# A Hymba layer on one core: a new first phase, a new order of products in the last unit, and new constants in the list scheduler

## The chip, the core and the metric

The kernel runs on one core of a Trainium2 chip. The core has five engines that run their own instruction lists in order and wait for each other by semaphores: TensorE (PE in the profile, with its weight loads as PEld), VectorE (DVE), ScalarE (ACT), GpSimd (POOL) and SyncE (SP), which here issues the transfers between the main memory and the on-chip memory. The metric is the device time of one execution in microseconds (us); the number for a kernel is the median of several executions.

## The reference

One decoder layer over 2048 tokens of width 1024, followed by a final RMS norm, all in float32. What matters of it:

```python
mod = silu(c) @ w_ada + b_ada
shift, scale, gate = split(mod, 3)
h = rmsnorm(x, g_norm) * (1 + scale) + shift
gq, gk, gv, ga, gz, sq, sk, sv, sz = split_cols(h @ w_in, COL_SIZES)
log_a = log_sigmoid(ga @ w_decay + b_decay) / 16
o_gla = rmsnorm(gla_chunked(gq, gk, gv, log_a), g_gla_head) * silu(gz)
o_swa = sliding_window_sink_attention(rope(sq), rope(sk), sv, sinks) * silu(sz)
x = x + gate * (concat(o_gla, o_swa) @ w_out)
return rmsnorm(x, g_final)
```

The first three lines are the modulation and the norm. `c` is one row, so `mod` is one row for all tokens. The projection by `w_in` is the largest piece of work; its columns are cut into slots named `sz`, `gz`, `kv`, `gv`, `sq` and `qk`.

## The kernel before, in words

**Tiling.** The 2048 tokens are four units of 512 (`NU`, `NB`). Within a unit the width of 1024 is eight blocks of 128 (`KT`, index k or j). Numbers are split into a high part, rounded to the format fp32r, and the low remainder, and one product becomes three: high by high, low by high, high by low. `hh` and `hl` are the two parts of the modulated, normed h; weights are split in the same way in unit 0, stored to a scratch tensor `wc`, and reloaded by the units 1 to 3. `mmul` (L454 in the profile) issues each matrix product and `trans` (L459) each transposition; a wrapper at L397 issues the operations of the other engines and the transfers.

**What sets the order.** The kernel does not issue directly. The class `Order` records each operation with a modelled duration; `issue` then takes, engine by engine, the operation that can start first by the model and, among those ready, the one with the smallest key. `od.lift` moves keys (a negative lift brings work forward). `begin` holds the model of time: when an engine is free, how fast the transfers (`wire`) go, and how far SyncE may run ahead. All operations of the whole kernel are sorted in this way, so a constant in `begin` can move instructions in any unit. The engines keep the order that comes out.

**The first phase** (unit 0). SyncE loads the small tensors, x transposed (`xT`, into `xt0`), the modulation's weights (`wa`, one tile for each k with a shift half and a scale half) and the first weights (`wr_first`). `warm` issues small products without use (`pw`). `silu_rows` spreads silu(c) over all partitions by 16 small products (`pb`). `norm0_start` squares the eight blocks of x on ScalarE and VectorE, adds them in pairs (`sq`), sums them over the partitions by four products with a matrix of ones (`ss`), and makes 1/rms by two ScalarE activations (log, then exp). The result stands in `ss`, and a copy of it in `rstd`. The second use of `warm` fills TensorE's time behind the sums. `ada_cols` multiplies `wa` by the silu row and adds along the row, on VectorE (two operations a k); ScalarE then makes `ashift` and `amul` of k. `norm0_scale` and `norm0_k` make `hh` and `hl` of one k. For k=1, 3, 5, 7 VectorE multiplies x by `amul` and `rstd` in one operation and ScalarE adds `ashift`. With each k that is finished, `proj_t_outer` issues the products of this k into open sums (`po`).

**The slots.** Each unit runs through a list of slots; `ORDER0` is that of unit 0, `ORDER` that of units 1 and 2, `ORDER_F[3]` that of unit 3 (`FAST` names the units with a fast form). Unit 3 makes `sq` and `gv` together, as slot `sqgv`, with seven block products in place of eight. `SEVEN` lists them, with the block of h or sum of blocks at the left and of the weights at the right: `slot_f` streams their weights (tiles `w_b` from `wc`, tiles `w_t` from sums of weight blocks made before and stored to `wt`), and `proj_f` issues the products (`pf`) and what follows each. The sums of blocks of h (`S`, split to `Shh` and `Shl`) are made by `prepare` and pass through a scratch tensor `sd` on the way. Attention work becomes ready when the slots that it needs are done.

**Late work.** The gate's third of the modulation and the output weights are made in small pieces behind slots of the units 1 and 2; `LATE_AT` says where.

Of the kernel before, what the change touches and what calls it, by code (L numbers as in the profile page):

```python
# [18 lines left out]
P = 128  # L19
# [38 lines left out]
FAST = (3,)  # L58
ORDER_F = {2: ['sz0','kv','sz1','sqgv','qk0','gz0','qk1','gz1'], 3: ['sz0','kv','sqgv','sz1','qk0','gz0','qk1','gz1']}
STATS_AT = 0  # L60
# [3 lines left out]
SEVEN = (("a11", "b11"), ("a12", "b21"), ("s2", "t2"), ("s3", "t3"), ("a22", "t4"), ("s1", "t1"), ("s4", "b22"))  # L64
LATE_AT = {(1,'sz0'):'gate',(1,'sz1'):0,(1,'sq'):4,(1,'gv'):5,(1,'qk1'):6,(2,'sz0'):7,(2,'sz1'):1,(2,'gv'):2,(2,'gz0'):3}
WO = ("b11", "b21", "t1", "b22", "t2", "t3", "t4")
WARM0, WARM = 14, 13
WITH_V = (1, 3, 5, 7)
# [37 lines left out]
class Order:  # L106
# [3 lines left out]
    def __init__(self, tc):  # L110
        self.tc, self.nc = tc, tc.nc
        self.real = {"V": self.nc.vector, "A": self.nc.scalar, "G": self.nc.gpsimd,
                     "PE": self.nc.tensor, "SP": self.nc.sync}
        self.ops, self.tiles, self.rings, self.seen = [], {}, {}, {}
        self.free = dict.fromkeys(self.real, 0.0)
        self.port = self.wire = 0.0
        self.mode = self.cell = None
        self.last = dict.fromkeys(self.real)
        self.busy = {}
        self.group, self.groups = None, 0  # L120
        self.lift = 0
        self.home, self.after_pool, self.users_of = {}, {}, {}
# [195 lines left out]
    def begin(self, o, t):  # L318
        e = o.eng
        if o.bytes:  # L320

            self.wire = max(self.wire, t + 0.9) + o.bytes / (360e3 if t < 20 else 370e3)
            o.start, o.end = t, max(self.wire + 0.9, t + 2.0)
            self.free[e] = max(t + 0.07, self.wire - BACKLOG)
            return
        if e == "PE":
            dur = o.dur
            if o.mode != self.mode:
                t += 0.1
# [73 lines left out]
def layer_kernel(ctx, tc, small, x, xT, w_ada, w_gate, b_gate, w_in, w_dec, w_out, g_fin, out):  # L403
# [37 lines left out]


    def mmul(o, l, r, start, stop, bank=None):
        n, m, k = free_size(r), free_size(l), l.shape[0]
        mode = cell = None
        if l.dtype == F32:
            dur = 2 * max(0.107, n / 1200)
            if k <= 64:
                mode, cell = "rows", l.start_partition()
            elif m <= 64:  # L450
                mode, cell = "cols", o.start_partition()
        else:
            dur = max(0.112, n / 2400 + 0.0137)
        return od.add("PE", lambda: T.matmul(o, l, r, start=start, stop=stop), dur,  # L454
                      [l, r] + ([] if start else [o]), [bank if start and bank is not None else o],
                      mode=mode, cell=cell)
# [84 lines left out]
    def silu_rows():  # L541

        pb = rows.tile([P, D], F32, name="pb")
        for j in range(KT):
            with od.together():
                for i in range(2):
                    mmul(pb[:, j * P:(j + 1) * P], s_p[i][:, j:j + 1].broadcast_to([P, P]), ident_r,
                         i == 0, i == 1)
        return pb

    def ada_load(j):
        wa = begin.tile([P, 2, D], F32, name=f"wa{j}", tag="wa", bufs=WAB)
        was[j] = wa
        if j == 0:
            for i in range(2):
                SY.dma_start(wa[:, i], w_ada[:, j, i])
# [136 lines left out]

    def slot_f(u):

# [15 lines left out]

        stream.extend([lambda n=n, j=j: load(n, j) for n in range(7) for j in range(2)])
        return lambda i, n, k: tiles[n, k // 2][:, k % 2, i]
# [38 lines left out]

    def proj_f(u, w, combos, qr_of):

# [53 lines left out]
        combos, second = combos  # L808
        for n, (a, _) in enumerate(SEVEN):
            if n == STATS_AT and u < NU - 1:  # L810
# [7 lines left out]
            for p in range(2):  # L818
# [6 lines left out]
                done(a, p, ps)  # L825
                od.lift = 0

    def rope_in_place(q, t):
# [159 lines left out]
    def norm0_start():  # L988
# [4 lines left out]
        for j in range(0, KT, 2):  # L993
# [658 lines left out]
    todo = [(0, n) for n in ORDER0] + [(u, n) for u in range(1, NU) for n in (ORDER_F[u] if u in FAST else ORDER)]  # L1652
    ws = [slot_f(u) if n == "sqgv" else slot_w(u, n, LIFT if i > 1 else 0) for i, (u, n) in enumerate(todo)]
    ready_s = {}

    warm(WARM0, None)
    srow = silu_rows()
    norm0_start()
    b1 = const.tile([P, KT], F32, name="b1")
# [54 lines left out]
    for i, (u, slot) in enumerate(todo):  # L1714
# [8 lines left out]
        elif name == "sqgv":  # L1723
            qrs[u] = {}
            proj_f(u, w, ready_s[u], qrs[u])
        elif name == "sq":
# [7 lines left out]
        seen.add((u, slot))  # L1734
        seen |= {(u, n) for n in ("sq", "gv") if name == "sqgv"}
        if half:
# [22 lines left out]
        if u < NU - 1 and name == ("sqgv" if u in FAST else NORM_AT if u else NORM_AT0):  # L1759
            od.lift = -LIFT  # L1760
# [66 lines left out]
```

## Time and profile before

| | us |
|---|---|
| median of 3 runs | 822.41 (822.4 to 823.12) |
| profiled execution, its own time | 822.16 |
| its span, first to last instruction | 820.4 |
| VectorE busy (76% of the span) | 626.8 |
| ScalarE busy (64%) | 528.0 |
| GpSimd busy (46%) | 377.7 |

The span is what the trace covers; the execution's own time holds 1.8 us more around it. The mean granted clock of TensorE is 0.998 over the span. The transfers move 221.79 MB at a mean of 270 GB/s. In a timeline row the first number is the start in the span, the second the time from the first start to the last end of the group, `xN` the number of instructions in it, and the bracket at the end says how long the engine idled before it and what released it. One product of 128x512 in float32 counts as two records.

### The profile page before, as it was taken

The numbers are of one execution on the slowest core, as the hardware profiler recorded it, in microseconds if no ns is written. First come the engines' busy times: TensorE is split into PE (matmuls) and PEld (weight loads), VectorE is DVE, ScalarE is ACT, GpSimd is POOL, SyncE is SP. The second block draws the span as 40 slices with busy tenths as digits, with TensorE's granted clock in tenths as the row PEclk, the third lists the DMA queues.
The fourth block names the chain that finished last, engine by engine and source line by source line (L and its number), as shares of the span: only waits on it lengthen the run. The fifth ranks groups of instructions, "written<-read, shape, count | busy, mean of one in ns | idle before, by whom it ended". The sixth has DMA issues, their size and how long they took to land.

```text
span 820.4 us, 13492 instructions
## 1 busy us (share of the span) xinstructions
PE 803.6 (98%) x4262; PEld 669.0 (82%) x4262; DVE 626.8 (76%) x1234; ACT 528.0 (64%) x1315; POOL 377.7 (46%) x458
## 2 busy tenths in 40 slices
PE   8899999999999999999999999999999999999996
PEld 7788788888888878878887888788888888888885
DVE  6998467777668988675788958877686577989985
ACT  4769856899546787857488766453786636444432
POOL 3813225476435766656569542343644332223300
PEclk9999999999999999999999999999999999999999
DMA  9979998738286597998977967899999945664422
GB/s 357 372 257 379 380 388 290 265 130 325 100 291 233 195 371 251 303 336 307 348 278 269 324 225 235 286 353 402 340 350 346 309 128 178 218 201 153 165 99 78
DMA packets 101917, 221.79 MB, mean 270 GB/s; under 512 B 10531, under 2 KB 28502, under 8 KB 99158
## 3 DMA queue, kind: packets, MB, share of 16 engines
q1 hardware_dynamic: 101558, 220.67, 75.8%
q8 instruction: 34, 0.56, 0.3%
q14 instruction: 37, 0.30, 0.1%
q10 hardware_dynamic: 288, 0.26, 0.1%
HBM read 156.80 MB, written 64.09 MB: 269 GB/s over the span
## 4 chain that ended last, share of the span: by engine, by line
PE 76%; DMA 7%; DVE 4%; ACT 4%; issue 2%; POOL 1%; SPq 1%; DVEq 0%; POOLq 0%; ACTq 0%
PE pt L454 23%; PE pn L454 15%; PE ya L454 10%; PE ys L454 9%; PE pf L454 5%; PE ppo L454 3%; PE psc L454 3%; PE po L454 2%; PE ppt L459 2%; DMA xt<-in_xT 1%; DMA xn<-in_x 1%; PE pc L454 1%; PE pms L454 1%; DMA wr_gv<-in_w_in 1%; PE pu L454 1%
## 5 line engine op out<-in xcount | busy, mean ns | idle before, releaser
L454 PE MATMUL pt<-hh,w_gz 128*128 128x512 f32 x224 | 75.7, 397 | 0.0
L454 PE MATMUL pt<-hh,w_qk 128*128 128x512 f32 x224 | 74.5, 398 | 0.0
L454 PE MATMUL pt<-hh,w_sz 128*128 128x512 f32 x224 | 73.6, 397 | 0.3 <-ACT kvr L397 0.3
L397 ACT ACTIVATE ge<-ge 128x512 f32<-128x512 f32 x96 | 60.5, 630 | 9.8 <-DVE ge L397 8.9
L397 ACT ACTIVATE s<-s,nm 128x129 f32<-128x129 f32 x128 | 51.1, 400 | 18.4 <-DVE nm L397 17.8
L454 PE MATMUL pn<-w_gv,hh 128*128 128x512 f32 x192 | 62.0, 397 | 0.2 <-ACT kvr L397 0.2
L454 PE MATMUL pn<-w_sq,hh 128*128 128x512 f32 x192 | 61.7, 395 | 0.0
L397 POOL TENSOR_TENSOR xt<-xt,rstd 128x512 f32<-128x512 f32 x27 | 40.6, 1505 | 28.7 <-DMA xt<-in_xT 24.9
L454 PE MATMUL ys<-woht,m 128*128 128x512 f32 x168 | 53.6, 392 | 0.0
L397 POOL TENSOR_TENSOR o<-o,zs 128x128 f32<-128x128 f32 x64 | 33.5, 542 | 39.8 <-DVE o L397 29.8
L454 PE MATMUL pn<-w_kv,hh 128*128 128x272 f32 x256 | 50.1, 290 | 0.2 <-ACT zs L397 0.2
L454 PEld LDWEIGHTS pt<-hh,w_sz 128*128 128x128 f32 x224 | 41.7, 188 | 9.2 <-ACT kvr L397 0.5
L454 PE MATMUL ya<-wohb,m 128*128 128x512 f32 x152 | 49.0, 390 | 0.0
L454 PEld LDWEIGHTS pt<-hh,w_gz 128*128 128x128 f32 x224 | 41.7, 188 | 8.5 <-issue 0.2
L454 PEld LDWEIGHTS pt<-hh,w_qk 128*128 128x128 f32 x224 | 41.7, 188 | 8.3
L397 POOL TENSOR_TENSOR s<-s,den 128x512 f32<-128x512 f32 x32 | 37.7, 1181 | 16.1 <-DVE den L397 15.3
L454 PE MATMUL pt<-hl,w_gz 128*128 128x512 f32 x112 | 44.5, 397 | 0.0
L454 PE MATMUL pt<-hl,w_sz 128*128 128x512 f32 x112 | 44.4, 396 | 0.0
L454 PE MATMUL pt<-hl,w_qk 128*128 128x512 f32 x112 | 44.3, 396 | 0.0
L397 POOL TENSOR_TENSOR qr<-qr,rope 128x256 f32<-128x256 f32 x32 | 26.4, 846 | 35.4 <-DVE rope L397 25.7
L454 PEld LDWEIGHTS pn<-w_sq,hh 128*128 128x128 f32 x192 | 35.8, 188 | 8.1 <-issue 0.3
L454 PEld LDWEIGHTS psc<-kst,qs 128*128 128x128 f32 x256 | 37.7, 188 | 5.5 <-DVE s L397 1.0
(324 smaller groups left out, 2475.1 us busy)
## 6 DMA issues: line engine op xcount, KB each, us to landing
w_sz<-wc SPq DMA_DIRECT2D x24, 512.0 KB, 6.2
w_qk<-wc SPq DMA_DIRECT2D x24, 512.0 KB, 5.1
w_gz<-wc SPq DMA_DIRECT2D x24, 512.0 KB, 5.1
w_sq<-wc SPq DMA_DIRECT2D x16, 512.0 KB, 7.0
w_gv<-wc SPq DMA_DIRECT2D x16, 512.0 KB, 9.1
w_t<-wt SPq DMA_DIRECT2D x16, 512.0 KB, 7.4
mr<-mixd SPq DMA_DIRECT2D x32, 256.0 KB, 3.6
y<-in_x SPq DMA_DIRECT2D x32, 256.0 KB, 3.3
```

Source lines behind the costliest of these rows:

```text
L397: return order.add(eng, lambda: real(*args, **kw), dur, ins, outs, lock=lock, nbytes=nbytes)
L454: return od.add("PE", lambda: T.matmul(o, l, r, start=start, stop=stop), dur, [l, r] + ([] if start else [o]), [bank if start and bank is ...
L459: return od.add("PE", lambda: T.transpose(o, i, ident), 0.109, [i, ident], [o], mode="few" if o.shape[0] <= 32 else None)
```

## The change

1. `WARM0` goes from 14 to 5 and `WARM` from 13 to 9. `FILL` puts two small products behind the silu row and behind each of the first three sums. In the planner these first products get longer durations (`cold`).
2. In `ada_load` and `ada_cols` the scale half stands ahead of the shift half, and `amul` follows its half at once.
3. The copy of 1/rms to `rstd` goes from ScalarE to VectorE.
4. The planner's constants: all engines are free from 0.8 us, the first load is costed by itself, the wire runs at 405 GB/s ahead of 20 us in place of 360, and an issue costs 0.45 us ahead of 6 us.
5. Unit 3: `sz1` comes ahead of `sqgv`, and `sqgv` keeps the first five of the seven products (`SPLIT`); the last two become a slot of their own, `gvb`, behind `qk0`. (`ORDER_F[2]` is changed too, but unit 2 is not in `FAST`.)
6. `LATE_AT`: the gate and the first output rows come in one slot, and five other pieces move to other slots of units 1 and 2.

```diff
-ORDER_F = {2: [...], 3: ['sz0','kv','sqgv','sz1','qk0','gz0','qk1','gz1']}
+ORDER_F = {2: [...], 3: ['sz0', 'kv', 'sz1', 'sqgv', 'qk0', 'gvb', 'gz0', 'qk1', 'gz1']}
-LATE_AT = {(1,'sz0'):'gate',(1,'sz1'):0,(1,'sq'):4,(1,'gv'):5,(1,'qk1'):6,(2,'sz0'):7,(2,'sz1'):1,(2,'gv'):2,(2,'gz0'):3}
+LATE_AT = {(1, 'sz0'): ('gate', 0), (1, 'kv'): 4, (1, 'gv'): 5, (1, 'qk1'): 6, (2, 'sz0'): 7, (2, 'kv'): 1, (2, 'qk0'): 2, (2, 'gv'): 3}
-WARM0, WARM = 14, 13
+WARM0, WARM = 5, 9
+FILL = (2,2,2,2)
...
-        self.free = dict.fromkeys(self.real, 0.0)
+        self.free = dict.fromkeys(self.real, 0.8)
...
-            self.wire = max(self.wire, t + 0.9) + o.bytes / (360e3 if t < 20 else 370e3)
+            if not self.wire:
+                self.wire = 2.8
+                o.start, o.end = t, t + 1.75
+                self.free[e] = t + 0.45
+                return
+            self.wire = max(self.wire, t + 0.9) + o.bytes / (405e3 if t < 20 else 370e3)
             o.start, o.end = t, max(self.wire + 0.9, t + 2.0)
-            self.free[e] = max(t + 0.07, self.wire - BACKLOG)
+            self.free[e] = max(t + (0.45 if t < 6 else 0.07), self.wire - BACKLOG)
...
+        od.lift = -LIFT
+        warm(FILL[0], x)
+        od.lift = 0
         return pb
...
         if j == 0:
-            for i in range(2):
+            for i in (1, 0):
                 SY.dma_start(wa[:, i], w_ada[:, j, i])
...
-        for i in range(2):
+        for i in (1, 0):
             V.scalar_tensor_tensor(wa[:, i], wa[:, i], 1.0, srow, op0=ALU.mult, op1=ALU.mult,
                                    accum_out=ada[:, j, i:i + 1])
-        A.activation(ashift[:, j:j + 1], ada[:, j, 0:1], AF.Identity, bias=b_sb[:, j, 0:1])
-        A.activation(amul[:, j:j + 1], ada[:, j, 1:2], AF.Identity, bias=b1[:, j:j + 1], scale=g_sb[:, j:j + 1])
+            if i:
+                A.activation(amul[:, j:j + 1], ada[:, j, 1:2], AF.Identity, bias=b1[:, j:j + 1],
+                             scale=g_sb[:, j:j + 1])
+            else:
+                A.activation(ashift[:, j:j + 1], ada[:, j, 0:1], AF.Identity, bias=b_sb[:, j, 0:1])
...
+    SPLIT = 5
+
+    def part_of(u, slot):
+        at = SPLIT if "gvb" in ORDER_F[u] else len(SEVEN)
+        return range(at) if slot == "sqgv" else range(at, len(SEVEN))
...
             i = mmul(ps, ones, sq[0], j == 0, j == KT - 2)
+            if j < KT - 2:
+                warm(FILL[1 + j // 2], i)
             od.lift = 0
...
-            od.lift = 60
-            A.copy(rstd[0], rstd[1])
-            od.lift = 0
+            V.tensor_copy(rstd[0], rstd[1])
...
+    cold[0] = 0.427
     warm(WARM0, None)
+    cold[0] = 0.17
     srow = silu_rows()
+    cold[0] = 0.0
     norm0_start()
```

What the planner makes of it is seen in the engines' lists. First TensorE's head: behind the first warm-up (one row, x14 before and x5 now) and the silu row's products (`pb`), before:

```order
L454 MATMUL pb<-ident_r,s_cl 128x128
L454 MATMUL ss<-sq_112,ones_r 128x512
L454 MATMUL ss<-sq_114,ones_r 128x512
L454 MATMUL ss<-sq_116,ones_r 128x512
L454 MATMUL ss<-sq_118,ones_r 128x512
L454 MATMUL pw<-ident,ones_r 128x128 x13
L454 MATMUL po_141<-hh_0_149,w_first_123 128x256
```

and now (`pw` are the small products, `ss` the sums; a product's line is L463 in the changed file):

```order
L463 MATMUL pb<-ident_r,s_cl 128x128
L463 MATMUL pw<-ident,ones_r 128x128 x2
L463 MATMUL ss<-sq_113,ones_r 128x512
L463 MATMUL pw<-ident,ones_r 128x128 x2
L463 MATMUL ss<-sq_116,ones_r 128x512
L463 MATMUL pw<-ident,ones_r 128x128 x2
L463 MATMUL ss<-sq_119,ones_r 128x512
L463 MATMUL pw<-ident,ones_r 128x128 x2
L463 MATMUL ss<-sq_122,ones_r 128x512
L463 MATMUL pw<-ident,ones_r 128x128 x9
```

The four sums had stood next to each other; now two small products stand ahead of each. In all there are 22 small products where there were 27.

Second, VectorE from the last pair of squares on, before (`wa` with `ada` is the modulation, two operations a k; the number behind `hl_` or `hh_` is k):

```order
L397 TENSOR_TENSOR sq_118<-sq_118,sq_119 128x512
L397 SCALAR_TENSOR_TENSOR wa_147,ada<-wa_147,pb 128x1024 x2
L397 TENSOR_TENSOR xt_111<-xt_111,ss 128x256 x2
L397 TENSOR_TENSOR hl_0_150<-xt_111,hh_0_149 128x256 x2
L397 SCALAR_TENSOR_TENSOR wa_151,ada<-wa_151,pb 128x1024 x2
L397 SCALAR_TENSOR_TENSOR xt_111<-xt_111,amul,rstd_121 128x512
```

and now:

```order
L403 TENSOR_TENSOR sq_122<-sq_122,sq_123 128x512
L403 SCALAR_TENSOR_TENSOR wa_151,ada<-wa_151,pb 128x1024 x2
L403 TENSOR_TENSOR xt_112<-xt_112,ss 128x256 x2
L403 COPY rstd_125<-ss 128x512
L403 SCALAR_TENSOR_TENSOR wa_155,ada<-wa_155,pb 128x1024 x2
L403 TENSOR_TENSOR hl_0_154<-xt_112,hh_0_153 128x256 x2
L403 SCALAR_TENSOR_TENSOR xt_112<-xt_112,amul,rstd_125 128x512
```

The copy has come in, and the modulation of k=1 has moved ahead of `hl` of k=0. On ScalarE the copy is gone, and `amul` of k=0 stands ahead of the two activations of 1/rms in place of behind them.

Third, SyncE in unit 3, from the loads of the products' first weights on, before (with the buffers' numbers: `S013` to `S313` are the four sums of h that are stored, `w_b113` and `w_b213` the weights of the first two products, `w_t23` those of the third, `w_sz13` those of slot `sz1`):

```order
L397 DMA w_b113_0_1407<-wc_102 128x1024 x2
L397 DMA sd3_104<-S013_1395 128x512
L397 DMA sd3_104<-S113_1397 128x512
L397 DMA w_b113_1_1432<-wc_102 128x1024 x2
L397 DMA w_b213_0_1433<-wc_102 128x1024 x2
L397 DMA w_b213_1_1434<-wc_102 128x1024 x2
L397 DMA sd3_104<-S213_1399 128x512
L397 DMA w_t23_0_1435<-wt_105 128x1024 x2
L397 DMA w_t23_1_1445<-wt_105 128x1024 x2
L397 DMA w_t33_0_1446<-wt_105 128x1024 x2
L397 DMA sd3_104<-S313_1401 128x512
L397 DMA S023_1465<-sd3_104 128x512
```

and now:

```order
L403 DMA sd3_104<-S013_1399 128x512
L403 DMA w_sz13_0_1411<-wc_102 128x1024 x2
L403 DMA sd3_104<-S113_1401 128x512
L403 DMA w_sz13_1_1436<-wc_102 128x1024 x2
L403 DMA w_b113_0_1437<-wc_102 128x1024 x2
L403 DMA sd3_104<-S213_1403 128x512
L403 DMA w_b113_1_1438<-wc_102 128x1024 x2
L403 DMA w_b213_0_1439<-wc_102 128x1024 x2
...
L403 DMA sd3_104<-S313_1405 128x512
L403 DMA S023_1477<-sd3_104 128x512
L403 DMA w_t23_0_1452<-wt_105 128x1024 x2
```

The weights of `sz1` have come ahead of those of the seven products, and the first `w_t` load has moved from ahead of the last store of S to behind it.

More of the change, by code (lines that the diff above doesn't have):

```diff
@@ L58 @@
 FAST = (3,)
-ORDER_F = {2: ['sz0','kv','sz1','sqgv','qk0','gz0','qk1','gz1'], 3: ['sz0','kv','sqgv','sz1','qk0','gz0','qk1','gz1']}
+ORDER_F = {2: ['sz0','kv','sqgv','sz1','qk0','gz0','qk1','gz1'], 3: ['sz0', 'kv', 'sz1', 'sqgv', 'qk0', 'gvb', 'gz0', 'qk1', 'gz1']}
 STATS_AT = 0
@@ L440, in f @@
         return ap.bitcast(F32)
+    cold = [0.0]
     def mmul(o, l, r, start, stop, bank=None):
@@ L453, in mmul @@
             dur = max(0.112, n / 2400 + 0.0137)
+        dur = max(dur, cold[0])
         return od.add("PE", lambda: T.matmul(o, l, r, start=start, stop=stop), dur,
@@ L462, in warm @@
     def warm(n, after):
+        if not n:
+            return
         p = att.tile([P, P], F32, name="pw", tag="pqk")
@@ L468, in warm @@
                 i.deps.add(after)
+        return i
     sm = const.tile([P, SMALL[-1]], F32, name="small")
@@ L546, in silu_rows @@
                 for i in range(2):
-                    mmul(pb[:, j * P:(j + 1) * P], s_p[i][:, j:j + 1].broadcast_to([P, P]), ident_r,
-                         i == 0, i == 1)
+                    x = mmul(pb[:, j * P:(j + 1) * P], s_p[i][:, j:j + 1].broadcast_to([P, P]), ident_r,
+                             i == 0, i == 1)
+        od.lift = -LIFT
+        warm(FILL[0], x)
+        od.lift = 0
         return pb
@@ L692, in late_cols, with slot_f @@
         part("t4", b[1, 0], b[1, 0], b[1, 1])
-    def slot_f(u):
+    SPLIT = 5
+    def part_of(u, slot):
+        at = SPLIT if "gvb" in ORDER_F[u] else len(SEVEN)
+        return range(at) if slot == "sqgv" else range(at, len(SEVEN))
+    def slot_f(u, slot):
         tiles = {}
@@ L710, in load @@
                 SY.dma_start(f(t[:, k]), f(src))
-        stream.extend([lambda n=n, j=j: load(n, j) for n in range(7) for j in range(2)])
+        stream.extend([lambda n=n, j=j: load(n, j) for n in part_of(u, slot) for j in range(2)])
         return lambda i, n, k: tiles[n, k // 2][:, k % 2, i]
@@ L751, in prepare, with proj_f @@
         return combos, second
-    def proj_f(u, w, combos, qr_of):
+    def proj_f(u, combos, qr_of):
         def left(op, k, p):
@@ L808, in proj_f, with product @@
         combos, second = combos
-        for n, (a, _) in enumerate(SEVEN):
+        def product(n, a, w):
             if n == STATS_AT and u < NU - 1:
@@ L826, in proj_f, with run @@
                 od.lift = 0
+        def run(slot, w):
+            for n in part_of(u, slot):
+                product(n, SEVEN[n][0], w)
+        return run
     def rope_in_place(q, t):
@@ L1652, in layer_kernel @@
     todo = [(0, n) for n in ORDER0] + [(u, n) for u in range(1, NU) for n in (ORDER_F[u] if u in FAST else ORDER)]
-    ws = [slot_f(u) if n == "sqgv" else slot_w(u, n, LIFT if i > 1 else 0) for i, (u, n) in enumerate(todo)]
-    ready_s = {}
+    ws = [slot_f(u, n) if n in ("sqgv", "gvb") else slot_w(u, n, LIFT if i > 1 else 0) for i, (u, n) in enumerate(todo)]
+    ready_s, run_f = {}, {}
+    cold[0] = 0.427
     warm(WARM0, None)
+    cold[0] = 0.17
     srow = silu_rows()
+    cold[0] = 0.0
     norm0_start()
@@ L1724, in layer_kernel @@
             qrs[u] = {}
-            proj_f(u, w, ready_s[u], qrs[u])
+            run_f[u] = proj_f(u, ready_s[u], qrs[u])
+            run_f[u](name, w)
+        elif name == "gvb":
+            run_f[u](name, w)
         elif name == "sq":
@@ L1734, in layer_kernel @@
         seen.add((u, slot))
-        seen |= {(u, n) for n in ("sq", "gv") if name == "sqgv"}
+        if name == "sqgv":
+            seen.add((u, "sq"))
+        last_f = u in FAST and name == ("gvb" if "gvb" in ORDER_F[u] else "sqgv")
+        if last_f:
+            seen.add((u, "gv"))
         if half:
@@ L1746, in layer_kernel @@
                               ("Z", 0, ("qk0", "gz0", "gv")), ("Z", 1, ("qk1", "gz1", "gv"))):
-            if (name in need or name == "sqgv") and all((u, n) in seen for n in need):
+            if (name in need or "sq" in need and name == "sqgv" or "gv" in need and last_f) and all((u, n) in seen for n in need):
                 if what == "S":
@@ L1758, in layer_kernel @@
                     od.lift = 0
-        if u < NU - 1 and name == ("sqgv" if u in FAST else NORM_AT if u else NORM_AT0):
+        if u < NU - 1 and (last_f if u in FAST else name == (NORM_AT if u else NORM_AT0)):
             od.lift = -LIFT
```

## The prediction

> **What bounds the kernel now.** I read the page's part on engines first, then TensorE's waits, then the table by windows, then the timelines of the stages to which the waits point.
>
> ```profile
> PE 803.6 (98%) x4262; PEld 669.0 (82%) x4262; DVE 626.8 (76%) x1234; ACT 528.0 (64%) x1315; POOL 377.7 (46%) x458
> PE po L454 <- ACT hh L397: 2.3, 2, 2.1
> PE pw L454 <- POOL ones_r L397: 2.1, 1, 2.1
> PE pf L454 <- DMA w_b<-wc: 1.7, 1, 1.7
> PE pk L459 <- DVE qk L397: 1.2, 1, 1.2
> 25.00:40.00 15.00, 15.00 (x68) 12.42 (x67) 14.77 (x24) 10.91 (x27) 12.48 (x14) 1.00 1.00 374
> 60.00:100.00 40.00, 38.89 (x214) 32.84 (x213) 26.02 (x59) 34.18 (x73) 12.52 (x22) 1.00 1.00 376
> ```
>
> The reader is to see that TensorE is busy for 803.6 of 820.4 us, so the kernel is little else than TensorE's list of products. The four waits (us in total, times, longest) are most of its idle time outside the tail. A change can gain in three ways only: fewer products on that list, an earlier start of its dense part, or a wait taken away. In the window rows TensorE, its weight loads, VectorE, ScalarE and GpSimd stand in that order, then the clock, the transfers' share and GB/s. From 25 to 40 us VectorE is busy for 14.77 of 15 us beside a full TensorE, so what delays VectorE there is soon felt. From 60 to 100 us the transfers' share is 1.00, and TensorE loses only 1.1 us.
>
> TensorE's first phase, from its timeline:
>
> ```profile
> 2.12 6.01 PE L454 MATMUL pw<-ident,ones_r 128*128 128x128 f32 x28 [2.12 <-POOL ones_r L397]
> 2.00:6.00 4.00, 3.88 (x18) 3.88 (x19) 1.93 (x10) 0.92 (x3) 0.36 (x2) 1.00 0.94 307
> 7.88 0.30 PE L454 MATMUL pb<-ident_r,s_ch 128*128 128x128 f32 x1
> 9.59 0.28 PE L454 MATMUL pb<-ident_r,s_cl 128*128 128x128 f32 x1
> 9.70 3.65 PE L454 MATMUL ss<-sq,ones_r 128*128 128x512 f32 x8
> 13.19 3.06 PE L454 MATMUL pw<-ident,ones_r 128*128 128x128 f32 x26
> 16.42 0.48 PE L454 MATMUL po<-hh,w_first 128*128 128x256 f32 x2 [0.17 <-ACT hh L397]
> 23.05 1.20 PE L454 MATMUL po<-hh,w_first 128*128 128x512 f32 x4 [2.10 <-ACT hh L397]
> 27.27 1.07 PE L454 MATMUL po<-hh,w_first 128*128 128x512 f32 x4
> ```
>
> A warm-up product is two passes (28 records for 14). Eighteen passes fill 3.88 us up to 6.0, so 0.216 us each. The silu row's 16 products come (9.59 - 7.88) / 15 = 0.114 us apart, the second warm-up's passes (3.06 - 0.28) / 25 = 0.111. So TensorE starts at half its pace, though the row's clock column says 1.00. The first 28 passes took 7.88 - 2.12 = 5.76 us; 25.3 at 0.216 and 2.7 at 0.111 make that, so the pace changed at about 7.6 us, 5.5 us after the first product. A sum of squares is two passes of (13.19 - 9.70) / 8 = 0.436 us. The dense part begins at 23.05 with the second outer product, k=1, and runs 27.27 - 23.05 = 4.2 us a k from there. What sets 23.05 is a chain of VectorE and ScalarE:
>
> ```profile
> 13.45 0.84 ACT L397 ACTIVATE rstd<-ss,eps_c 128x256 f32<-128x256 f32 x2 [2.01 <-PE ss L454]
> 15.16 0.75 DVE L397 TENSOR_TENSOR xt<-xt,ss 128x256 f32<-128x256 f32 x2 [0.71 <-ACT ss L397]
> 17.29 0.92 DVE L397 TENSOR_TENSOR hl<-xt,hh 128x256 fp32r<-128x256 f32 x2 [1.38 <-ACT xt L397]
> 17.66 0.57 ACT L397 COPY rstd<-ss 128x512 f32<-128x512 f32 x1
> 18.13 1.21 DVE L397 SCALAR_TENSOR_TENSOR wa<-wa,pb 128x1024 f32<-128x1024 f32 x1
> 19.27 1.22 DVE L397 SCALAR_TENSOR_TENSOR wa<-wa,pb 128x1024 f32<-128x1024 f32 x1
> 20.53 0.39 ACT L397 ACTIVATE amul<-ada,b,small 128x1 f32<-128x1 f32 x1 [0.55 <-DVE wa L397]
> 20.95 1.30 DVE L397 SCALAR_TENSOR_TENSOR xt<-xt,amul,rstd 128x512 f32<-128x512 f32 x1 [0.46 <-ACT amul L397]
> 22.28 0.72 ACT L397 ACTIVATE hh<-xt,ashift 128x512 fp32r<-128x512 f32 x1 [1.36 <-DVE xt L397]
> ```
>
> VectorE idles 1.38 us for ScalarE's xt and 0.46 us for amul, and hl of k=0 and both halves of the modulation stand between.
>
> **The first phase after the change.** TensorE's head becomes 5 warm-ups, the silu row, then two small products ahead of each sum. Step by step from 2.12: 10 passes at 0.216 end at 4.28; the 16 row products, still at the slow pace, end at 7.73; four fills of 4 passes at 0.111 are 1.78; four sums are 8 x 0.436 = 3.49. The sums end at 13.00, against 13.19: 0.19 earlier. Trading nine warm-ups for eight fills thus saves almost nothing by itself. What it saves hangs on the pace: the five products taken out (10 passes) are cheap ones.
>
> From there I move the chain. Rstd's two activations and the scaling of xt shift by 0.19, so VectorE ends xt at 15.91 - 0.19 = 15.72. The copy of rstd is new on VectorE, and no row shows it; ScalarE's own took 0.57, and I take 0.6 (bounds 0.5 and 0.9, VectorE's 128x512 row of two operands just above). It ends at 16.3. Now k=1's two modulation rows stand ahead of hl instead of behind it, 1.14 us apart, so they take 16.3 to 18.6. The scale half is first, hence amul is done long before it is wanted, and the 0.46 us wait goes. The hl pair takes 0.84 (17.29 to 18.13), so to 19.45, with ScalarE's xt ready by 17.6. Then xt 1.30 to 20.75, hh at 20.78, and TensorE 0.77 later (22.28 to 23.05): **k=1 at 21.55 instead of 23.05, a gain of 1.5 us**. The copy on VectorE costs its 0.6 in this sum, and hides the wait for ScalarE's xt. TensorE has no work in the hole either way.
>
> Does the data come in time? The loads of the modulation give these rows:
>
> ```profile
> 4.89 0.45 SPq L397 DMA_DIRECT2D wa<-in_w_ada  x1
> wa<-in_w_ada SPq DMA_DIRECT2D x7, 1024.0 KB, 10.4
> 45.45 0.35 SPq L397 DMA_DIRECT2D wr_gz<-in_w_in  x1
> ```
>
> Issued at 4.89, 10.4 us to landing: 15.3 for k=1, ahead of 16.3. If the sums ended more than 1 us earlier still, this landing would bind. Later k's follow on TensorE at 4.2 us each, with VectorE moved by the same 1.5 us. At 45.45 the queue resumes when VectorE frees the raw weights, so the transfers' stretch from 45 to 100 us moves with it. I keep the full 1.5 us, with losses of up to 1 us there as a bound.
>
> The pace is the uncertain part. If it changed at 5.5 us instead of 7.6, the sums would end at 11.9, the landing at 15.3 would bind and k=1 start at 20.65 (-2.4). If at 8.9, the fills and the first sum would be slower by 0.6, and the gain 0.9.
>
> The Trainium skill, page "TensorE: Matmul & The Clock Gate", section "Part 1: The HAM clock gate", speaks to that row. It says that TensorE runs at half clock until it has been busy through a window of about 3.4 us, and that this window runs freely, so that the change varies from run to run and is a matter of time and not of the number of products. The trace agrees with the two paces (0.216 and 0.111) and with 5.5 us, which lies between one window and two. By that rule the change falls from 2.1 + 3.4 = 5.5 to 2.1 + 6.8 = 8.9, an estimate from the page, and the gain is 0.9 to 2.4; by the row alone it is 1.5.
>
> **Unit 3.** Its first product of seven waits for its weights:
>
> ```profile
> 505.64 10.43 SPq L397 DMA_DIRECT2D sd<-S  x2
> 516.16 3.34 SPq L397 DMA_DIRECT2D w_b<-wc  x6
> 533.24 0.32 SPq L397 DMA_DIRECT2D sd<-S  x1
> 518.52 0.62 PE L454 MATMUL pf<-w_b,hh 128*128 128x512 f32 x2
> 522.24 0.73 PE L454 MATMUL pf<-w_b,hh 128*128 128x512 f32 x2 [1.71 <-DMA w_b<-wc]
> 532.78 0.62 PE L454 MATMUL pf<-w_t,Shh 128*128 128x512 f32 x2
> w_t<-wt SPq DMA_DIRECT2D x16, 512.0 KB, 7.4
> ```
>
> The SP queue works in order. Its second store of S waits on VectorE until 516.07, and the w_b loads stand behind it, while the products begin at 518.52. After the change the slot sz1 stands first: 48 products of 4.2 / 18 = 0.233 us, 11.2 us of work whose first tile of weights is queued ahead of the blocked store and whose second is not wanted for 5.6 us. The w_b loads are then issued at about 517 and wanted at 529.7, so **the 1.71 us wait goes**; bounds 0 to -1.9 (with the slower restart around it). The next in line is w_t. It is now queued behind the last store of S, issued at 533.24 before, so issued at about 534.6 and, at 7.4 us, landed near 542. It is wanted 532.78 - 518.52 - 1.71 = 12.55 us after w_b's start, at about 542. That is even, with some products of the attention between to help; a later S would reopen the wait.
>
> **The rest of the order.** Every engine's list is re-sorted by the planner's new times, and the late gate and output-weight slots move in units 1 and 2. No product is added but the fills: 5 warm-ups fewer in all. One wait of unit 2 could go or grow:
>
> ```profile
> 353.95 0.63 ACT L397 ACTIVATE xn<-xn 128x512 f32<-128x512 f32 x1 [2.89 <-DMA xn<-in_x]
> 358.15 0.66 PE L459 MATMUL pk<-ident,qk 128*128 128x128 f32 x4 [1.20 <-DVE qk L397]
> ```
>
> ScalarE waits in order for a row of x whose load stands behind weights, the decay behind it comes late, and TensorE waits 1.2 us for qk. In the new order the same squares still stand ahead of the decay and the load still behind a tile of w_sz. I cost it at nothing, bounds -1.2 and +1.5. The cover is the product slot around it; without it the whole 2.89 us would show.
>
> **The sum.** -1.5 (first phase) - 1.7 (unit 3) + 0 = -3.2, on the profiled execution's 822.16, so 819.0. That execution stands 0.25 below the median of 822.41; on the median it is **819.2**.
>
> **Rivals.**
> - One of the two gains is given back. Either w_t lands 2 us late and takes over w_b's wait, or the transfers bind between 45 and 100 us and swallow the earlier start. For it: the even reckoning at 542, and the share of 1.00. Against it: only 1.1 us of TensorE's time is lost in 40 us there. Then 822.4 - 1.6 = 820.8.
> - The change does not do what it says: the sums' end moves by only 0.19 us, and if VectorE's copy and the earlier modulation rows meet a late wa or a late xt, k=1 stays near 23, and unit 3's wait only moves. Then 822 to 822.4. For it: nothing in the TensorE list got shorter by more than 10 passes. Against: 1.38 + 0.46 us of VectorE's idle time in the chain are visibly free to use.
> - Slower: the half pace lasts through the sums, since the first phase now holds fewer products ahead of them. The fills would be 3.5 and the sums 7.0, ending at 18.2; k=1 at 26.7, or +3.7, and +7 if k=0's products were slow as well. The point from which it costs is a change of pace 3 us later than now, about 10.6, since each us longer adds half a us to a margin of 1.5. Against: TensorE has no hole before the sums, so it is as busy as before. With unit 3's gain it gives 824.4.
>
> **Chances.** The forecast (both gains, within 1.5) 0.58; one gain 0.20; none 0.09; slower pace 0.08; a new wait of the 2.89 us kind in the re-sorted units, with gains lost, 0.05. Faster by over 0.2% (1.64 us, about what a measurement of this kernel can tell from no change) takes the first and nearly half of the second: 0.67. Same: the rest of the second, the third and part of the fifth, 0.22. Slower: 0.11. The range reaches from -2.4 - 1.9 - 1.2 = -5.5 at best, of which I keep 817.0, up to 822.6, which leaves the slow pace and half of the new waits out.
>
> **What would show it.** Right: the sums end near 13.0, k=1's first product stands near 21.5, no wait of pf for w_b, and sz1's products right behind kv in unit 3. Wrong: records of pw and ss at 0.216 and 0.87 beyond 8 us, a wait of pf for w_t above a us, a larger wait of pk, or TensorE's idle time between 45 and 100 us up by the 1.5 us that the start won.

## The result, and the profile after

The change made the kernel slower: a median of 829.51 us (825.77 to 831.08, 5 runs) beside 822.41 before (5 runs), a ratio of 1.008 with an interval of 1.0057 to 1.0104. The profiled execution took 830.53 us with a span of 828.6. The forecast was 819.2.

The lines of the page and of TensorE's waits that answer to those shown of before, for the changed kernel:

```profile
PE 806.3 (97%) x4252; PEld 668.9 (81%) x4252; DVE 628.9 (76%) x1235; ACT 528.8 (64%) x1314; POOL 374.1 (45%) x458
PE pw L463 <- POOL ones_r L403: 2.1, 1, 2.1
PE po L463 <- ACT hh L403: 2.1, 2, 1.1
PE pn L463 <- ACT kvr L403: 1.8, 2, 1.6
PE ppo L463 <- POOL pp L403: 1.6, 1, 1.6
PE pk L468 <- DVE qk L403: 1.2, 1, 1.2
PE ppo L463 <- ACT ph L403: 1.1, 1, 1.1
PE psc L463 <- DVE s L403: 1.1, 1, 1.1
```

TensorE's idle time went from 820.4 - 803.6 = 16.8 us to 828.6 - 806.3 = 22.3. The wait for `w_b` is gone from the list, as forecast. In its place stand new waits, each of a us or two, for ScalarE, GpSimd and VectorE: `kvr`, `pp`, `ph`, `s`. Before, waits for `kvr` and `s` were 0.3 us at most and the list had none for `pp` and `ph`. The other 806.3 - 803.6 = 2.7 us of the longer span are in TensorE's busy time, which holds the slow pace of the first phase and also every wait that is shorter than the tail of the product before it.

The table by windows shows where. Two stretches of before, then four of the changed kernel (the first number behind the comma is TensorE's busy time):

```profile
150.00:200.00 50.00, 49.77 (x297) 43.90 (x298) 41.08 (x95) 47.34 (x140) 32.21 (x48) 1.00 0.59 204
200.00:250.00 50.00, 50.00 (x280) 41.56 (x279) 31.48 (x69) 28.89 (x76) 22.46 (x35) 1.00 0.63 228
```

```profile
150.00:200.00 50.00, 47.27 (x275) 40.03 (x274) 36.78 (x80) 43.22 (x128) 28.30 (x41) 1.00 0.55 175
200.00:250.00 50.00, 48.86 (x268) 40.05 (x268) 33.68 (x76) 30.38 (x77) 26.46 (x39) 1.00 0.61 219
400.00:450.00 50.00, 48.89 (x247) 39.82 (x246) 42.62 (x78) 34.60 (x97) 32.04 (x36) 1.00 0.75 264
500.00:550.00 50.00, 50.00 (x305) 43.23 (x304) 37.64 (x87) 29.79 (x60) 17.16 (x21) 1.00 0.80 270
```

From 150 to 250 us, in unit 1, TensorE idles 2.7 and 1.1 us where it idled 0.2 and 0 before, and from 400 to 450 us 1.1. No engine beside it is full (the busiest, ScalarE, 43.22 of 50 us, less than its 47.34 before); the transfers' share is 0.55 and 0.61. So neither an engine nor the wire binds there: engines wait for each other. Around unit 3, from 500 to 550, TensorE is full.

The first phase of the changed kernel, from TensorE's timeline:

```profile
7.73 1.16 PE L463 MATMUL pw<-ident,ones_r 128*128 128x128 f32 x4
8.69 1.91 PE L463 MATMUL ss<-sq,ones_r 128*128 128x512 f32 x2
10.39 0.82 PE L463 MATMUL pw<-ident,ones_r 128*128 128x128 f32 x4
11.04 1.02 PE L463 MATMUL ss<-sq,ones_r 128*128 128x512 f32 x2
14.52 2.17 PE L463 MATMUL pw<-ident,ones_r 128*128 128x128 f32 x18
23.39 1.20 PE L463 MATMUL po<-hh,w_first 128*128 128x512 f32 x4 [0.99 <-ACT hh L403]
```

The first sum's row is 1.91 us long, the second's 1.02: the pace changed only near 10.8 us, and the second fill took 11.04 - 10.39 = 0.65 in place of 0.44. The sums end at 14.5 and not at 13.0, and k=1 starts at 23.39, 0.34 later than before. That is a small part of 7 us.

### The profile page after: what moved, and what is told of

It is laid out like the page before. It is cut to its first block, busy times and chain, and to the rows that moved or that the text cites. A ratio compares the mean times of both kernels' runs of the same rounds, so it can differ in the third digit from the quotient of the medians.

```text
span 828.6 us, 13494 instructions
## 1 busy us (share of the span) xinstructions
PE 806.3 (97%) x4252; PEld 668.9 (81%) x4252; DVE 628.9 (76%) x1235; ACT 528.8 (64%) x1314; POOL 374.1 (45%) x458
## 4 chain that ended last, share of the span: by engine, by line
PE 71%; DVE 10%; ACT 7%; DMA 7%; issue 3%; SPq 1%; POOL 1%; DVEq 0%; ACTq 0%; POOLq 0%
PE pt L463 19%; PE pn L463 15%; PE ya L463 10%; PE ys L463 9%; PE pf L463 3%; PE psc L463 3%; PE ppo L463 2%; PE po L463 2%; DMA mixd<-o 2%; DVE wa L403 2%; DMA xn<-in_x 2%; SPq L403 1%; DVE hl L403 1%; PE pc L463 1%; PE ppt L468 1%
## 5 line engine op out<-in xcount | busy, mean ns | idle before, releaser
L463 PE MATMUL pt<-hh,w_qk 128*128 128x512 f32 x224 | 74.7, 399 | 0.0
L463 PE MATMUL pt<-hh,w_gz 128*128 128x512 f32 x224 | 74.0, 396 | 0.0
L463 PE MATMUL pt<-hh,w_sz 128*128 128x512 f32 x224 | 72.3, 395 | 0.7 <-ACT kvr L403 0.7
L403 ACT ACTIVATE ge<-ge 128x512 f32<-128x512 f32 x96 | 60.6, 631 | 12.6 <-DVE ge L403 11.4
L463 PE MATMUL pn<-w_gv,hh 128*128 128x512 f32 x192 | 62.7, 398 | 0.0
L463 PE MATMUL pn<-w_sq,hh 128*128 128x512 f32 x192 | 60.9, 394 | 0.0
L403 POOL TENSOR_TENSOR xt<-xt,rstd 128x512 f32<-128x512 f32 x27 | 36.4, 1350 | 39.2 <-DMA xt<-in_xT 35.6
L463 PE MATMUL ys<-woht,m 128*128 128x512 f32 x168 | 53.4, 392 | 0.0
L463 PE MATMUL pn<-w_kv,hh 128*128 128x272 f32 x256 | 50.1, 291 | 1.8 <-ACT kvr L403 1.8
L463 PEld LDWEIGHTS pt<-hh,w_sz 128*128 128x128 f32 x224 | 41.5, 188 | 9.5 <-ACT kvr L403 0.9
L463 PE MATMUL ya<-wohb,m 128*128 128x512 f32 x152 | 49.2, 392 | 0.0
L463 PEld LDWEIGHTS pt<-hh,w_gz 128*128 128x128 f32 x224 | 41.6, 188 | 8.7 <-issue 0.2
L463 PEld LDWEIGHTS pt<-hh,w_qk 128*128 128x128 f32 x224 | 41.6, 188 | 7.8
L403 POOL TENSOR_TENSOR s<-s,den 128x512 f32<-128x512 f32 x32 | 35.0, 1093 | 27.9 <-DVE den L403 25.4
L463 PEld LDWEIGHTS psc<-kst,qs 128*128 128x128 f32 x256 | 39.2, 188 | 8.1 <-DVE s L403 2.1
L463 PE MATMUL psc<-kst,qs 128*128 128x256 f32 (+1 forms) x256 | 44.1, 287 | 1.2 <-DVE s L403 1.1
L463 PE MATMUL pt<-hl,w_sz 128*128 128x512 f32 x112 | 44.3, 395 | 0.7 <-DVE hl L403 0.7
L463 PE MATMUL pt<-hl,w_qk 128*128 128x512 f32 x112 | 44.3, 396 | 0.0
L403 DVE TENSOR_TENSOR o<-ppo,o 64x256 f32<-64x256 f32 x64 | 26.9, 421 | 22.7 <-ACT o L403 21.8
L463 PE MATMUL pt<-hl,w_gz 128*128 128x512 f32 x112 | 44.1, 394 | 0.0
```

Of the source, the lines that this page charges most:

```text
L403: return order.add(eng, lambda: real(*args, **kw), dur, ins, outs, lock=lock, nbytes=nbytes)
```

## The experiments

Theory A: the loss comes from the lists, which the planner re-sorted from the first phase to unit 3. Theory B: it comes from the new first phase itself. To part the two, some kernels below hold the order: each recorded operation gets a number, and `issue` no longer plans but follows a table of these numbers, taken from another kernel's list and edited only where the text says so.

```diff
-        while left:
-            best = None
...
-        out.sort(key=lambda o: (o.start, o.idx))
+        rank = {s: i for i, s in enumerate(TABLE)}
+        out = sorted(self.ops, key=lambda o: rank[o.sid])
```

Every ratio is to the kernel before on the same chip in the same series. Its medians there were 823.23 us in the first series, 822.35 in the second and 822.83 in the third. Where a difference in us is given by the ratio, it is that share of these times; the difference of the medians can be another by up to a us.

**First phase alone, all else held.** The table is that of before; edited are only the rows of the first phase, to the places that they have in the changed kernel.

```diff
-WARM0, WARM = 14, 13
+WARM0, WARM = 5, 9
+FILL = (2,2,2,2)
...
-            for i in range(2):
+            for i in (1, 0):
...
-            A.copy(rstd[0], rstd[1])
+            V.tensor_copy(rstd[0], rstd[1])
```

> All edits of the first phase (5 and 9 small products with 2 between, scale half first, copy on VectorE, modulation of k=1 ahead of hl), with the rest of every engine's list held as it was before. Theory A (the loss comes from the re-sorted lists of the units 0 to 2): k=1 starts between 20.6 and 23.4 us by TensorE's pace, and the time is 820 to 823 us. Theory B (the new first phase itself costs, through its slow pace or what it delays): about 828 to 830 us, with the new waits of TensorE at 74, 172 and 435 us back.

Measured: 821.87 us, ratio 0.9985 (0.997 to 1.0). Theory B falls. TensorE's waits in this run:

```profile
PE pw L752 <- POOL ones_r L692: 2.1, 1, 2.1
PE pk L757 <- DVE qk L692: 1.4, 2, 1.2
PE po L752 <- ACT hh L692: 1.1, 1, 1.1
PE pf L752 <- DMA w_b<-wc: 0.7, 2, 0.5
PE pn L752 <- ACT zs L692: 0.7, 1, 0.7
```

and its windows in unit 1:

```profile
150.00:200.00 50.00, 49.90 (x298) 43.59 (x297) 39.87 (x95) 46.51 (x138) 31.09 (x46) 1.00 0.59 204
200.00:250.00 50.00, 50.00 (x280) 41.60 (x279) 31.73 (x70) 28.66 (x77) 22.71 (x35) 1.00 0.64 231
```

TensorE is full where it idled 2.7 and 1.1 us, and the waits for `pp`, `ph` and `kvr` of 1 us and more are not there, though in this trace the pace changed only near 11.4 us and k=1 began at 23.64, as late as in the changed kernel.

**The changed lists with the first phase of before.** The mirror image: the table of the changed kernel, with the first phase's rows set back.

```diff
-WARM0, WARM = 5, 9
-FILL = (2,2,2,2)
+WARM0, WARM = 14, 13
+FILL = (0,0,0,0)
...
-            for i in (1, 0):
+            for i in range(2):
...
-            V.tensor_copy(rstd[0], rstd[1])
+            A.copy(rstd[0], rstd[1])
```

> The changed kernel's lists throughout, but the first phase as it was before (14 and 13 small products, copy on ScalarE, shift half first). Theory A: the loss stays, 827 to 831 us. Theory B: the loss goes, and with unit 3's wait for w_b gone too the time is about 821 us.

Measured: 828.5 us, ratio 1.0075 (1.0057 to 1.0093). The loss stays with the lists. In its trace k=1 starts at 21.86, 1.2 us earlier than in the first one of before, and that does not help.

**Unit 3's order alone**, sorted by the planner (the lists up to unit 3 come out as before):

```diff
-ORDER_F = {2: [...], 3: ['sz0','kv','sqgv','sz1','qk0','gz0','qk1','gz1']}
+ORDER_F = {2: [...], 3: ['sz0', 'kv', 'sz1', 'sqgv', 'qk0', 'gvb', 'gz0', 'qk1', 'gz1']}
```

> The kernel before with unit 3's new order of slots alone (sz1 ahead of the first five products, the last two behind qk0); the lists of units 0 to 2 are those of before. Both theories: the wait for w_b goes and no wait for w_t comes, 820.7 us, 1.7 below before. Rival: the last two products behind qk0 delay the attention, and the time is at or above 823 us.

Measured: 820.88 us, ratio 0.9982 (0.9968 to 0.9996), so 1.5 us by the ratio (the medians differ by 2.35). `pf` waits for no load in its trace. In the changed kernel too, neither `w_b` nor `w_t` is waited for; the rows of SyncE and of TensorE there:

```profile
525.32 0.85 SPq L403 DMA_DIRECT2D w_b<-wc  x2
540.26 0.86 SPq L403 DMA_DIRECT2D w_t<-wt  x2
539.06 0.39 PE L463 MATMUL pf<-w_b,hh 128*128 128x512 f32 x1
555.39 0.61 PE L463 MATMUL pf<-w_t,Shh 128*128 128x512 f32 x2
```

The first `w_b` is issued 13.7 us ahead of its product and `w_t` 15.1, so the rival that `w_t` takes over the wait fell; from the first product with `w_b` to the first with `w_t` are 16.3 us, where I had counted 12.55, and the queue was clear of the blocked store in time.

**The modulation's part alone, all else held** (with the 14 and 13 small products of before, and the modulation of k=1 ahead of `hl`):

```diff
-            for i in range(2):
+            for i in (1, 0):
...
-            A.copy(rstd[0], rstd[1])
+            V.tensor_copy(rstd[0], rstd[1])
```

> Only the modulation's part of the first phase (scale half first, copy on VectorE, modulation of k=1 ahead of hl), with the 14 and 13 small products of before and every other list held. If the gain worked out for this chain is right and the pace is what failed, TensorE's pace changes near 7.6 us, k=1 starts at 21.7 us and the time is 821.0 us. If the dense part of the first phase takes the gain back (VectorE or the loads bind), it is within 0.4 us of before.

Measured: 821.55 us, ratio 0.9981 (0.9965 to 0.9997); k=1 at 22.01 in its trace.

**Which cause of the re-sort?** Three kernels change one thing each and let the planner sort. The late work's places alone (beside the first output rows, which join the gate, four pieces move; "five" in the list of the change is one too many):

```diff
-LATE_AT = {(1,'sz0'):'gate',(1,'sz1'):0,(1,'sq'):4,(1,'gv'):5,(1,'qk1'):6,(2,'sz0'):7,(2,'sz1'):1,(2,'gv'):2,(2,'gz0'):3}
+LATE_AT = {(1, 'sz0'): ('gate', 0), (1, 'kv'): 4, (1, 'gv'): 5, (1, 'qk1'): 6, (2, 'sz0'): 7, (2, 'kv'): 1, (2, 'qk0'): 2, (2, 'gv'): 3}
```

> The kernel before with only the places of the late gate and output-weight work changed (LATE_AT); the lists are the same up to the first of these places in unit 1. Theory A1 (the moved late work carries the loss: it crowds VectorE, ScalarE and the transfers of units 1 and 2): 826 to 830 us. Theory A2 (the planner's constants carry it) or A3 (any re-sort of units 0 to 2 costs about as much): A2 821 to 824, A3 825 to 828 us.

Measured: 832.04 us, ratio 1.0112 (1.0095 to 1.013). The constants alone:

```diff
-        self.free = dict.fromkeys(self.real, 0.0)
+        self.free = dict.fromkeys(self.real, 0.8)
...
-            self.wire = max(self.wire, t + 0.9) + o.bytes / (360e3 if t < 20 else 370e3)
+            self.wire = max(self.wire, t + 0.9) + o.bytes / (405e3 if t < 20 else 370e3)
```

(with the rest of the change's lines in `begin`)

> The kernel before with only the planner's constants changed (engines free from 0.8 us, first load by itself, 405 GB/s and 0.45 us an issue early); nothing is added to or taken from the work, all lists from unit 0 on are re-sorted. A1: 821 to 824 us. A2: 826 to 830 us. A3: 825 to 828 us.

Measured: 828.87 us, ratio 1.0073 (1.0047 to 1.0099). The first phase's edits, sorted by the planner in place of held:

```diff
-        rank = {s: i for i, s in enumerate(TABLE)}
-        out = sorted(self.ops, key=lambda o: rank[o.sid])
+        while left:
+            best = None
...
```

> All edits of the first phase, as in the run with the other lists held, but sorted by the planner with the constants of before: the lists of all units come out otherwise. Against that run (821.9 us) the difference is the re-sort alone. A1 and A2: 821 to 824 us. A3: 825 to 828 us.

Measured: 835.56 us, ratio 1.016 (1.0135 to 1.0186). The same edits with the lists held took 821.87. All three lie above the kernel before, each with a list of its own, so A1 and A2 (one part carries the loss) fall and A3 stands in kind. Its size was too small: all three lie above its 825 to 828 us. The sizes are not equal, and two of the three are larger than the loss of the whole change: the parts do not add. Their waits differ as well. The largest of the last run:

```profile
PE pt L458 <- ACT kvr L398: 2.8, 2, 1.5
PE psc L458 <- DVE s L398: 2.3, 1, 2.3
PE pf L458 <- ACT Shl L398: 2.1, 1, 2.1
```

**One number of the model.** The sharpest test of A3, since it touches no work:

```diff
-            self.wire = max(self.wire, t + 0.9) + o.bytes / (360e3 if t < 20 else 370e3)
+            self.wire = max(self.wire, t + 0.9) + o.bytes / (380e3 if t < 20 else 370e3)
```

> The kernel before with one number of the planner's model changed: 380 in place of 360 GB/s for the first 20 us. No work is added, moved by hand or taken away; the lists of all units come out otherwise. If any re-sort costs (A3), 825 to 835 us. If the loss is special to the constants and late work of the change, 821 to 824 us.

Measured: 829.13 us, ratio 1.0081 (1.0063 to 1.0098), as much as the whole change. One of its new waits, from the timelines of TensorE and ScalarE, with two windows of the table:

```profile
73.75 0.52 PE L454 MATMUL pn<-w_kv,hh 128*128 128x272 f32 x2 [2.18 <-ACT kvr L397]
69.56 1.28 ACT L397 ACT_TABLE_LOAD   x1
72.02 1.28 ACT L370 ACT_TABLE_LOAD   x1
73.32 0.39 ACT L397 COPY kvr<-pn 128x272 f32<-128x272 f32 x1
23.94:27.36 3.42, 2.87 (x7) 2.31 (x8) 3.42 (x6) 2.59 (x7) 3.42 (x4) 0.50 1.03 419
75.14:78.55 3.41, 3.41 (x18) 3.41 (x17) 0.81 (x5) 0.30 (x1) 1.95 (x3) 0.50 1.03 404
```

The clock column (the third number from the end) reads 0.50 in both windows: behind this wait, and with one of 3.25 us ahead of k=1, TensorE's clock was halved for 3.41 us. That is up to 1.7 us of its work each, an estimate from the two numbers. The changed kernel's trace has no such stretch between its first phase and its tail, and the mean clock of its executions is 0.998 to 0.999, against 0.994 in all four here. So the two kernels do not lose in the same way, and that they lose the same amount is chance; what this run shows is that a new order alone can cost that much.

**Two rows moved.** The same row stood in the way in the changed kernel. Its ScalarE and GpSimd, with what TensorE waited for:

```profile
70.22 1.28 ACT L403 ACT_TABLE_LOAD   x1
72.69 1.28 ACT L376 ACT_TABLE_LOAD   x1
73.98 0.39 ACT L403 COPY kvr<-pn 128x272 f32<-128x272 f32 x1
74.42 0.52 PE L463 MATMUL pn<-w_kv,hh 128*128 128x272 f32 x2 [1.62 <-ACT kvr L403]
172.17 1.27 POOL L403 TENSOR_TENSOR xt<-xt,rstd 128x512 f32<-128x512 f32 x1 [2.08 <-DMA xt<-in_xT]
173.40 1.09 POOL L403 TENSOR_SCALAR_AFFINE_SELECT pp<-pl 128x512 fp32r<-128x512 f32 x1
174.54 0.50 PE L463 MATMUL ppo<-pp,vd 128*128 128x512 f32 x1 [1.65 <-POOL pp L403]
```

The sine and cosine, with a table load on each side, stand ahead of the copy that frees TensorE's bank. And one block of x, whose load lands late, stands ahead of the masking that TensorE's next product needs. Before, two copies of `kvr` stood ahead of the table load, the second of them right in front of it:

```profile
69.56 0.39 ACT L397 COPY kvr<-pn 128x272 f32<-128x272 f32 x1
69.97 1.28 ACT L397 ACT_TABLE_LOAD   x1
```

The experiment moves the copy ahead of the sine and cosine in the changed kernel's table, exchanges the masking with the block of x, and moves no other row:

```diff
+L403 COPY kvr_249<-pn1_246 128x272
 L403 ACT_TABLE_LOAD
 L403 ACTIVATE sin_107<-rr0_228 128x512
 L403 ACTIVATE cos_106<-rr0_228 128x512
 L376 ACT_TABLE_LOAD
-L403 COPY kvr_249<-pn1_246 128x272
...
+L403 AFFINE_SELECT pp1_403<-pl_401 128x512
 L403 TENSOR_TENSOR xt1_7_560<-xt1_7_560,rstd1_493 128x512
-L403 AFFINE_SELECT pp1_403<-pl_401 128x512
```

> The changed kernel with two pairs of rows exchanged and no other row moved: on ScalarE the copy of the second kv block ahead of the sine and cosine (with their table loads), on GpSimd one masked block of the attention (pp of pl) ahead of the x block whose load lands late. If single rows ahead of work that waits are the mechanism, TensorE's waits of 1.6 us at 74 us and of 1.65 us at 174 us go, and the time falls by 2 to 3.5 us, to about 826.5 us. If the waits come from the engines' load as a whole, others take their place and it stays at 828 to 830 us.

Measured: 826.78 us, ratio 1.0048 (1.003 to 1.0067), against 829.51 and 1.008 for the changed kernel. Both waits are gone from TensorE's list. The rows of ScalarE and GpSimd now:

```profile
68.20 0.38 ACT L696 COPY kvr<-pn 128x272 f32<-128x272 f32 x1
68.60 1.28 ACT L696 ACT_TABLE_LOAD   x1
167.46 1.07 POOL L696 TENSOR_SCALAR_AFFINE_SELECT pp<-pl 128x512 fp32r<-128x512 f32 x1 [0.15 <-DVE pl L696]
169.26 1.28 POOL L696 TENSOR_TENSOR xt<-xt,rstd 128x512 f32<-128x512 f32 x1 [0.73 <-DMA xt<-in_xT]
```

So single rows can carry the loss: two out of several thousand were worth about 2.7 us by the medians. The two kernels were measured in different series and the intervals of their ratios overlap a little, so the size is rough; the 4.4 us that are left were not followed row by row. The pace changed at 5.9 us in this trace and k=1 began at 21.30, so of the profiled span's 4.0 us part is the pace.

**What is left of the change.** The small products alone, held:

```diff
-WARM0, WARM = 14, 13
+WARM0, WARM = 5, 9
+FILL = (2,2,2,2)
```

> Only the new small products (5, then 2 ahead of each sum, then 9), everything else held as before. By the sum in the prediction they are worth 0.19 us by themselves: within 0.5 us of before. If fewer of them ahead of the silu row keep the slow pace longer, k=1 starts later than 23.05 us when the pace changes after 8 us; if the pace changes by chance, it may fall on either side.

Measured: 823.87 us, ratio 1.0014 (1.0001 to 1.0026). They gain nothing; in this trace the pace changed near 11 us and k=1 began at 24.55. Then two combinations with all other rows held, with the table of the run with unit 3's order alone. First all edits of the first phase with unit 3's order:

```diff
-ORDER_F = {2: [...], 3: ['sz0','kv','sqgv','sz1','qk0','gz0','qk1','gz1']}
+ORDER_F = {2: [...], 3: ['sz0', 'kv', 'sz1', 'sqgv', 'qk0', 'gvb', 'gz0', 'qk1', 'gz1']}
...
-WARM0, WARM = 14, 13
+WARM0, WARM = 5, 9
+FILL = (2,2,2,2)
```

> All edits of the first phase and unit 3's new order, with every other row of the lists held as before. If the two gains seen apart (1.4 and 2.3 us) add up, 3.7 below before: 818.7 to 819.5 us. If they overlap (the start's gain being taken back behind the transfers), no better than unit 3 alone, about 2.3 below.

Measured: 820.54 us, ratio 0.9976 (0.9961 to 0.9991). And the same without the small products:

```diff
-WARM0, WARM = 5, 9
-FILL = (2,2,2,2)
+WARM0, WARM = 14, 13
+FILL = (0,0,0,0)
```

> The same without the new small products: 14 and 13 as before, only the modulation's part (scale half first, copy on VectorE, modulation of k=1 ahead of hl) and unit 3's order, the rest held. Gains of 1.7 and 2.3 us add up to 4.0: about 818.5 us. If the new small products are worth anything, it is slower than the run with them.

Measured: 820.23 us, ratio 0.9967 (0.9953 to 0.9981), 2.7 us below before by the ratio: the fastest by ratio of all that were run, and faster than both kernels. The two cannot be told apart. Each is a little less than the sum of its parts, and neither came down to what was expected of it.

## Why the prediction was wrong

**The step that failed is "The rest of the order".** It says that every engine's list is re-sorted, and then: "I cost it at nothing, bounds -1.2 and +1.5". The runs put the re-sort at 0.73% to 1.12% where the cause of it was a constant or the place of late work, and at 835.56 against 821.87 us where the same first phase was once planned and once held. I had seen that the order changed on all engines up to unit 3, and looked at one wait in it, that for `pk`. That wait stayed at 1.2 us, as written; the loss came at rows that I had not followed, such as the table load and the late block of x: in the changed kernel's trace the waits behind those two were 1.62 and 1.65 us, and moving the two rows returned about 2.7 of the 7.1 us. The rival that came true, "a new wait of the 2.89 us kind in the re-sorted units, with gains lost", had 0.05.

Why a re-sort should lose in each of the five planned lists that differ from before in units 0 to 2 (the change and four experiments) is not shown. What is shown is that the profile offered no cover: before, TensorE idles 9.6 us ahead of its last product, some 5 us of it outside the first phase. A list with so little idle time should have little to win by a new order and much to lose; that is an argument, not a run. The bounds of -1.2 and +1.5 were drawn from a single wait. In the traces of the four experiments, though not of the change, there are also stretches at half pace that came with a long wait (see the last section), so part of their loss may be that.

**The first phase: right in its chain, off in its sizes.** With the pace changing at 7.2 us, the held modulation gave k=1 at 22.01 against my 21.55 for 7.6. The copy took what I assumed, but the `hl` pair took longer, as in the changed kernel's VectorE:

```profile
17.16 0.68 DVE L403 COPY rstd<-ss 128x512 f32<-128x512 f32 x1
17.76 1.21 DVE L403 SCALAR_TENSOR_TENSOR wa<-wa,pb 128x1024 f32<-128x1024 f32 x1
20.04 1.34 DVE L403 TENSOR_TENSOR hl<-xt,hh 128x256 fp32r<-128x256 f32 x2
21.30 1.23 DVE L403 SCALAR_TENSOR_TENSOR xt<-xt,amul,rstd 128x512 f32<-128x512 f32 x1
```

Copy to modulation is 0.60, as taken; `hl` to the next row is 1.26, not 0.84. The term of 1.5 us measured 0.15% to 0.19%, 1.2 to 1.6 us by the ratio, in the held runs. The small products were costed at 0.19 us of gain and measured 0.14% of loss. And the pace itself left my bounds of 5.5 to 8.9 us: in the profiled execution it changed at 10.8.

**Unit 3: right.** The wait of 1.71 us went, no other wait for a load took its place, and alone the new order was worth 0.18%, 1.5 us. **The sum of the named parts**, -3.2, measured -2.0 us by the ratio, held together (0.9976; the forecast lies at the edge of its interval). So the parts that I worked out stand; the part that I left at nothing decided.

The slower rival, the slow pace through the sums, was not the cause: with the rest held, the profiled execution, with the late pace of 11.4 us and k=1 at 23.64, took 822.67 us, and the median of ten was 821.87. The rival that the transfers bind from 45 to 100 us was not tried by itself, but the trace of the modulation's part alone speaks against it. There k=1 starts 1.04 us earlier than before, and the first product of slot `sq` still 1.6 us earlier (104.00 against 105.60). About 1 us of the lead goes at 149.61, where TensorE waits 1.28 us for GpSimd's `s`, a wait of 0.24 us before.

## What to carry to other kernels

Where a planner sets the order, a change of its constants or of any early duration is a second change, of every list; price it apart, by holding the old order and applying the edit by hand, before judging either. In a kernel whose main engine is 98% busy, a fresh order is a risk of many small waits, and its bounds come from how many rows stand ahead of something that this engine needs, not from one wait. Where a new order is wanted, look in the waits' list for releasers that are new, and follow each back to the row that stood in front: moving two rows here returned about a third of the loss. A wait that is long enough can also cost more than itself, as the last section shows.

## What the runs showed of the hardware that was not expected

**The slow pace at the start varies by up to 6 us between executions.** It ended at 5.0 to 8.4 us in the eight traces that begin with 14 small products, and at 5.9 (two traces) or 10.8 to 11.4 (four traces) in the six that begin with 5 and then the silu row. The first product stands at 2.1 in all. So the slow stretch lasts 2.9 to 6.2 us with the one beginning, and 3.8 or 8.7 to 9.3 with the other. The Trainium skill, page "TensorE: Matmul & The Clock Gate", section "Part 1: The HAM clock gate", has the change depend on a free-running window of about 3.4 us and not on the number of products; two such windows would end at 8.9 us here, an estimate from the page's figure. Four traces lie beyond that, all with few small products ahead of the silu row. Counted back from the change in steps of 3.41 us (the next paragraph has the step), each of the four has one step filled almost by the row's products alone that passed without the change (3.99 to 7.41 us in the changed kernel, whose next step ended with the change at 10.82). Whether the row's products count for less is open; it was not tried by itself. The profile's clock column reads 1.00 during this slow stretch: the first record of the clock in each trace stands at the change, and the column counts the time ahead of it as full.

**A wait of about 2 us can bring the slow pace back.** Later in the kernel the clock column does show it:

```profile
22.10:25.50 3.40, 3.40 (x9) 2.64 (x10) 3.40 (x8) 2.81 (x7) 3.40 (x5) 0.50 1.03 420
289.25:292.60 3.35, 3.35 (x10) 2.57 (x9) 2.46 (x5) 3.31 (x10) 0.84 (x1) 0.50 0.63 161
```

The first row is from the run with unit 3's order alone, behind a wait of 2.08 us ahead of k=1; the second from the first phase's edits sorted by the planner, behind a wait of 2.31 us for `s`. In the 14 traces ten waits of TensorE between its first product and its tail are longer than 2 us. With seven of them came a clock of 0.50 for 3.41 us, with an eighth (2.77 us, the late work's places alone) for 6.83 us. Two had none: the kernel before's own wait of 2.10 us ahead of k=1 and one of 2.12 us. No shorter wait had one. Within a trace all changes of the clock lie a whole number of 3.413 us apart. Laid over these steps, the slow stretches came where 2.0 us or more of one step were idle; of the two waits without one, at most 1.8 us lay in one step. So a wait's place among the steps, which differs between executions, decides as well as its length.

**The spread of executions is wide.** The kernel before ran from 820.13 to 825.69 us in 25 executions of one series and from 821.04 to 827.11 in 29 of another. Differences of 1 to 2 us, as in the three runs of first-phase edits held, rest on ten executions each; one of these intervals reaches 1.0 and the two others only just exclude it.
